# A hybrid encoder layer with expert retrieval: second token tile preloaded, ScalarE copies reordered, value sums on GpSimd for one stage, every fourth value block split

## The chip, the cores and the metric

One core of a Trainium2 chip runs the whole program. The metric is device time in microseconds (us) of one execution; the figure for the kernel before is the median of three runs. Engines are named as the profile names them: PE is TensorE (PEld its weight load), DVE is VectorE, ACT is ScalarE, POOL is GpSimd, SP is SyncE, which here only issues DMAs. "f32r" is a rounded form of float32; the kernel makes one float32 product from three f32r products of rounded parts and remainders.

## The reference, cut to what matters

The layer runs on two inputs of 256 tokens, `x_prompt` and `x_sample`: a short convolution and attention, then a retrieval over 16,384 experts, each a row `u` and a row `v` of 1024 numbers. The part that the change touches is the retrieval:

```python
def peer_ffn(x, wq, subkeys, u_tab, v_tab):
    q = (xf @ wq).reshape(T, PEER_HEADS, 2, PEER_HALF)
    s = jnp.einsum('thpc,hpnc->thpn', q, subkeys)
    sv, si = lax.top_k(s, PEER_TOPK)
    ...
    gates = jax.nn.softmax(cv, axis=-1)
    uc = jnp.take(u_tab, ic, axis=0)
    a = jax.nn.gelu(jnp.einsum('thkd,td->thk', uc, xc)) * gc
    vc = jnp.take(v_tab, ic, axis=0)
    return jnp.einsum('thk,thkd->td', a, vc)
```

Each token takes 8 heads x 16 experts = 128 experts. The result is added to the token's row `h`.

## The kernel before, in words

**Two ways to the same sum.** For `x_prompt` the kernel gathers: for each of two tiles of 128 tokens ("tile 1" is `t == 0`, "tile 2" is `t == 1`) and each of the 128 choices `k`, `g_issue` (L151) has POOL issue an indirect DMA of 128 rows `u|v`, 8 KB each (1.05 MB), into one of four ring places (`grow`). `g_dot` (L180) multiplies the u half with the tile's `x` row and sums it (DVE, 128x1024), `g_weight` (L171) puts Gelu and the gate on the sum (ACT, two operations on `dots`), `g_val` (L162) adds weight times v half to the tile's `h` row (DVE, 128x1024). That makes 256 gathers. A place is free for the next gather when its `g_val` is done. For `x_sample` the kernel is dense: it computes all 16,384 experts with matmuls and multiplies with a gate matrix that is mostly zero.

**Stages in order of the program.** (1) Layer front of `x_prompt`, its query projection and top-k. (2) Layer front of `x_sample`, with the first gathers beside it. (3) `projections` (L342) for `x_sample`, the "query projection": per head, two groups of 8 matmuls `pqq`, key scores `pn`, and `step1` (L815), which does the head's top-k on DVE, with sums of pairs (`cd`, L256 to L263) on POOL. (4) The "expert stage" (L913): 128 blocks `j`, each a 512 KB load of `u`, 8 matmuls into `pSj`, Gelu on ACT, which also frees the PSUM tile (four of them, `psS`). Beside it runs the generator `gates_dense` (L848): it finishes top-k, transposes the picks (`pi`, `pg`), then 64 times builds one-hot matrices for 4 tokens (DVE `oi`, `oj`, `gh`, ACT `gl`), multiplies them (`pgm`) and puts the gates into the matrix `A` (`Al`, `Ah`): where block `j` is done, DVE multiplies, where not, ACT copies. (5) The "value stage" (L939): 128 blocks, each a 512 KB load of `v` and 4 matmuls of 512 columns into `acc`; then the result is added to `h` and stored.

**What paces the gathers.** `bg(us)` (L221) is called after each group of matmuls and adds a share of `us` to a credit; 2.65 of credit (`GU`) buys one call of `gather` (L194), which does the oldest dot, an older value sum and the next issue. The shares are `SF` in stage 2, `SR` in stage 3 (through `step1`), `SS` in stage 4, where `SBS` is the share of `gates_dense`. In stage 5 what is left is spread evenly over the blocks. Each issue also waits for the last matmul emitted before it (`pe_mark`). The pacing is arithmetic on constants: it hands out 22, 18, 110 and 106 gathers to stages 2 to 5.

**What is where.** Weights, `u` and `v` come through SP's queue in program order, into four places `wtile` (and two more, `vp`, for every third `v`). The `x` and `h` rows of tile 1 stand in tiles `xg` and `hg` of the pool `gc`; when tile 1's last dot and last sum are done, POOL loads tile 2's rows into the same places (L189, L166 to L168). A scheduler under the tile framework decides the final order on each engine; each engine then runs its list in order, so whatever stands behind a waiting instruction waits as well.

Of the kernel before, what the change touches and what calls it, by code (L numbers as in the profile page):

```python
# [38 lines left out]
SR = 0.6  # L39
SS = 0.64  # L40
SMAX = 0.7
SBS = 0.42
# [3 lines left out]
def encoder_layer(ctx: ExitStack, tc: tile.TileContext, xp, xs_, meta, vec, w_in, w_out, wq,  # L46
# [33 lines left out]
    wp = ctx.enter_context(sb("wp", 4))  # L80
    selp = ctx.enter_context(sb("sel", 1, "right"))
    gc = ctx.enter_context(sb("gc", 1, "right"))
    ga = ctx.enter_context(sb("ga", GBUF, "right"))
# [21 lines left out]

    def wtile(name):
        return wp.tile([P, D], F32, tag="w", name=name)

    def weights(src, s, split=False):

        w = [wtile("w").rearrange("p (c n) -> p c n", c=4) for _ in range(2)]
        for q in range(2):
            nc.sync.dma_start(w[q], src[:, s, 4 * q:4 * q + 4])
        if not split:
            return lambda c, k=0: w[c // 4][:, c % 4]
        hl = [ga.tile([P, 2 * D], F32R, tag="g", name=n).rearrange("p (q x) -> p q x", q=2) for n in ("whi", "wlo")]
# [32 lines left out]
    ring = [ga] * GBUF  # L149
# [30 lines left out]
    def g_dot():  # L180
# [7 lines left out]
        if t == 0 and k == P - 1:  # L188
            x = gc.tile([P, D], F32, tag="xg", name="xg1")  # L189
            pool.dma_start(x, xdram)  # L190
            gctx["x"] = x
# [242 lines left out]
    def front(s, h, rn):  # L434
# [286 lines left out]
        if s == 0:  # L721
            for t in range(2):
                x = gc.tile([P, D], F32, tag="xg", name="xg0") if t == 0 else tmp.tile([P, D], F32, tag="xs", name="xs")
                dve.scalar_tensor_tensor(x, h[:, t, :], rn[:, t:t + 1], gf, op0=ALU.mult, op1=ALU.mult)
                xs2.append(x)
            gctx["x"] = xs2[0]
        if s == 0:
            hg = gc.tile([P, D], F32, tag="hg", name="hg0")
            pool.tensor_copy(hg, h[:, 0, :])
            gctx["h"] = hg  # L730
# [107 lines left out]

    share.update(a=SR, b=0.0)
    projections(xr1, sk1, sc1, q1, step1, rescale=rescale)  # L840
    pfs.close()
# [6 lines left out]
    def gates_dense():  # L848
# [4 lines left out]
        topk_left[0] = -1  # L853
        ogx = ExitStack()
# [7 lines left out]
        for t in range(2):  # L862
# [14 lines left out]
            for o in range(P // OC):  # L877
# [12 lines left out]
                for q in range(OC // 4):  # L890
# [8 lines left out]
                    for part, lo, hi in ((Al, 0, JH), (Ah, JH, P)):  # L899
                        m = min(max(n, lo), hi)  # L900
# [3 lines left out]
                        if m < hi:  # L904
                            act.activation(part[:, m - lo:hi - lo, a:a + 4], pj[:, m:hi], AF.Copy, scale=1.0 / GSH)
# [6 lines left out]
    ut = {}  # L912
    for j in range(P):  # L913
# [7 lines left out]
        n = tau[0]  # L921
        if n:
            act.activation(p[:, :n], p[:, :n], AF.Gelu)
            dve.tensor_tensor(A(j)[:, :n], p[:, :n], A(j)[:, :n], op=ALU.mult)
        if n < 256:
            act.activation(A(j)[:, n:], p[:, n:], AF.Gelu)
        r_done[0] = j + 1
        bg(3.5)
    run_tasks()

    vp = ctx.enter_context(sb("vp", 2, "right"))
# [4 lines left out]
    hd_ = gc.tile([P, 2, D], F32, tag="xr", name="hd")  # L936
    left = len(queue) + len(pend)
    done = 0
    for j in range(P):  # L939
        vb = vp.tile([P, D], F32, tag="v", name="v") if j % 3 == 2 else wtile("v")  # L940
        nc.sync.dma_start(vb, vn3[:, j])
        if j == P // 2:
            for t in range(2):
                act.dma_start(hd_[:, t, :], hdram[1 + t])
        for t in range(2):
            for q in range(2):
                i = pe.matmul(acc[t][q], A(j)[:, t * P:(t + 1) * P], vb[:, q * 512:(q + 1) * 512],  # L947
                              start=j == 0, stop=j == P - 1, skip_group_check=True)
        pe_mark[0] = i
        want = left * (j + 1) // (P - 2)  # L950
        while done < want:
            gather()
            done += 1
    while queue or pend or vals:
        gather()
# [73 lines left out]
```

## Time and profile before

| | us |
|---|---|
| median of three runs (1370.44 to 1372.22) | 1370.68 |
| the profiled execution | 1362.99 |
| its span | 1360.9 |
| PE busy in the span | 1298.1 |
| DVE busy | 1031.9 |
| ACT busy | 437.4 |
| POOL busy | 414.0 |

The profile is one execution. Its page gives busy time by engine and by group of instructions; views of the trace give the same for a stretch ("windows"), the waits ("who waited for whom"), the DMA traffic and the instructions in order of time. PE reaches 95% of the span, but the DMA engines are full for long stretches too, so what counts is which of them ends last in which stage. A plain float32 matmul shows as two records.

### The profile page before, as it was taken

To read this page: it belongs to the slowest core of one execution; us is meant where nothing else is said; L and a number is where in the kernel's file an instruction comes from. 1 tells how busy PE (TensorE), PEld (TensorE's weight loads), DVE (VectorE), ACT (ScalarE), POOL (GpSimd) and SP (SyncE) were. 2 spreads that over 40 slices of the span, in tenths; PEclk is the share of its full clock that TensorE was granted. 3 is DMA by queue.
4 is the path that set the end of the run, shared out by engine and by line. 5 is a ranking of instruction groups with operands and counts; after the bars stand their busy time and mean duration, and the time that the engine had idled before them with its cause. 6 is when DMAs were issued, how large, how long until landed. Compare 5 with 4: busy or idle time off the path is not lost. (4 is left out here: it accounts for less than half of the span.)

```text
span 1360.9 us, 17663 instructions
## 1 busy us (share of the span) xinstructions
PE 1298.1 (95%) x5870; PEld 927.9 (68%) x5870; DVE 1031.9 (76%) x2356; ACT 437.4 (32%) x1467; POOL 414.0 (30%) x480
## 2 busy tenths in 40 slices
PE   5999998998999887999999999999999999999998
PEld 5888986677888666888888888774443344444443
DVE  5656999776999889988888996676666665666665
ACT  4555533732221312555555543111111111111111
POOL 2111224331344342222221221223455523433331
PEclk9999999999999998999999999999999999999999
DMA  6434637577998999999999999999999999999997
GB/s 218 126 109 153 206 107 263 199 272 301 366 341 332 390 399 374 348 368 367 355 368 359 366 375 376 377 416 416 417 417 417 418 416 417 416 417 416 416 417 294
DMA packets 90234, 460.19 MB, mean 338 GB/s; under 512 B 10512, under 2 KB 11024, under 8 KB 57120
## 3 DMA queue, kind: packets, MB, share of 16 engines
q0 software_dynamic: 37296, 270.02, 49.7%
q1 hardware_dynamic: 50832, 182.33, 36.1%
q10 hardware_dynamic: 2016, 6.72, 1.3%
q8 instruction: 46, 0.75, 0.2%
q14 instruction: 44, 0.36, 0.1%
HBM read 454.81 MB, written 4.19 MB: 337 GB/s over the span
## 5 line engine op out<-in xcount | busy, mean ns | idle before, releaser
L157 POOL DMA_INDIRECT grow<-in_uv,eidx x256 | 331.9, 1297 | 694.8 <-PE acc L947 118.1
L130 PE MATMUL pSj<-xr,u 128*128 128x256 f32 x2048 | 465.6, 385 | 12.6 <-ACT Al L63 10.5
L130 PEld LDWEIGHTS pSj<-xr,u 128*128 128x128 f32 x2048 | 386.3, 192 | 68.7 <-ACT Al L63 14.5
L63 DVE SCALAR_TENSOR_TENSOR grow<-grow,xg 128x1024 f32<-128x1024 f32 x256 | 312.5, 1221 | 143.6 <-DMA grow<-in_uv,eidx 138.6
L63 DVE SCALAR_TENSOR_TENSOR hg<-grow,dots,hg 128x1024 f32<-128x1024 f32 x256 | 327.9, 1281 | 77.4 <-ACT dots L63 67.9
L947 PE MATMUL acc<-v,Al 128*128 128x512 f32 x752 | 329.9, 596 | 1.8
L947 PEld LDWEIGHTS acc<-v,Al 128*128 128x128 f32 x752 | 140.6, 190 | 190.6 <-issue 164.2
L63 ACT ACTIVATE dots<-dots 128x1 f32<-128x1 f32 x256 | 51.6, 202 | 552.2 <-DVE grow L63 551.2
L947 PE MATMUL acc<-v,Ah 128*128 128x512 f32 x272 | 118.0, 594 | 0.2
L947 PEld LDWEIGHTS acc<-v,Ah 128*128 128x128 f32 x272 | 51.3, 190 | 66.7 <-issue 62.1
L63 ACT ACTIVATE gl<-oj,glo 128x128 f16<-128x128 f16 x256 | 88.8, 393 | 10.9 <-DVE oj L63 5.1
L63 ACT ACTIVATE dots<-dots,gate_all 128x1 f32<-128x1 f32 x256 | 75.1, 294 | 7.5 <-ACT dots L63 0.6
L63 DVE TENSOR_TENSOR wlo<-w,whi 128x1024 fp32r<-128x1024 f32 x42 | 51.0, 1217 | 19.9 <-ACT whi L63 13.9
L63 ACT ACTIVATE pSj<-pSj 128x256 f32<-128x256 f32 (+39 forms) x94 | 26.6, 284 | 110.7 <-PE pSj L130 110.7
L130 PE MATMUL pqq<-xr,w 128*128 128x256 f32 x256 | 59.5, 385 | 0.7 <-DMA w<-in_wq 0.7
L130 PEld LDWEIGHTS pqq<-xr,w 128*128 128x128 f32 x256 | 48.2, 194 | 7.3 <-DMA w<-in_wq 1.1
L63 ACT ACTIVATE whi<-w 128x1024 fp32r<-128x1024 f32 x42 | 43.9, 1055 | 20.5 <-PE pqq L130 9.5
L130 PE MATMUL pc<-xT,w 128*128 128x258 f32 (+1 forms) x192 | 47.5, 390 | 1.1 <-DVE rb L63 0.6
L130 PEld LDWEIGHTS pc<-xT,w 128*128 128x128 f32 x192 | 34.9, 192 | 8.6 <-issue 2.5
L130 PE MATMUL pqq<-xr,whi 128*128 128x256 f32 x128 | 37.2, 292 | 0.0
L130 PE MATMUL pqq<-xrl,whi 128*128 128x256 f32 x128 | 36.4, 285 | 0.3 <-DVE xrl L63 0.3
L894 PE MATMUL pgm<-gh,oi 128*128 128x128 f16 x256 | 35.5, 219 | 1.3 <-DVE gh L63 1.3
(268 smaller groups left out, 1539.3 us busy)
## 6 DMA issues: line engine op xcount, KB each, us to landing
u<-in_u_t SPq DMA_DIRECT2D x128, 512.0 KB, 6.8
v<-in_v_n SPq DMA_DIRECT2D x128, 512.0 KB, 14.9
w<-in_w_in SPq DMA_DIRECT2D x36, 512.0 KB, 4.3
w<-in_wq SPq DMA_DIRECT2D x32, 512.0 KB, 5.0
w<-in_w_out SPq DMA_DIRECT2D x16, 512.0 KB, 4.8
grow<-in_uv,eidx POOLq DMA_INDIRECT x256, 9.2
hdram<-h ACTq DMA_DIRECT2D x3, 512.0 KB, 3.0
h<-in_xp SPq DMA_DIRECT2D x2, 512.0 KB, 7.3
```

Source lines behind the costliest of these rows:

```text
L63: i = f(*a, **k)
L130: i = pe.matmul(out, st_(c, a), mv(c, b), start=(n == 0), stop=(n == NC * len(terms) - 1))
L157: i = pool.indirect_dma_start(out=r, out_offset=None, in_=uv, in_offset=bass.IndirectOffsetOnAxis(ap=eidx[:, t, k:k + 1], axis=0))
L894: pe.matmul(pg[:, r, :], oi[:, k, :], gh[:, k, :], start=True, stop=False)
L947: i = pe.matmul(acc[t][q], A(j)[:, t * P:(t + 1) * P], vb[:, q * 512:(q + 1) * 512], start=j == 0, stop=j == P - 1, skip_group_check=True)
```

## The change

- Tile 2's rows: the ring gets five places of 8 KB. One, `ga[0]`, first holds tile 1's `x` and `h`; when the first gather of tile 2 is issued, a free ring place is taken for tile 2's `x` and `h`, POOL loads them there, and `ga[0]` joins the ring. `xg` and `hg` go.
- Stage 3: `SR` goes from 0.6 to 0.7. The value sum becomes two operations: ACT scales the v half in place by the weight, POOL adds it to the `h` row.
- Stage 4: `SBS` goes from 0.42 to 0.38, and a `yield 4.0` stands ahead of the transposes. Gelu and product of block `j` are emitted after the matmuls of block `j + 1`. In `gates_dense` both ACT copies are emitted ahead of both DVE products.
- Stage 5: `v` comes in pairs of blocks (1 MB, 8 KB a row) into three places, which take the room of `wtile`. Every fourth block (`SPL`) is split: ACT rounds its `A` and `v` to f32r, DVE makes the two remainders, and PE does three f32r products in place of one float32 product. The `h` rows of `x_sample` are loaded after the last `v`, by SP, in place of halfway, by ACT.

The pacing arithmetic now hands out 22, 21, 109 and 104 gathers to stages 2 to 5.

```diff
-SR = 0.6
+SR = 0.7
-SBS = 0.42
+SPL = 4
+SBS = 0.38
...
+    def row_pair():
+        p = ring_free.pop(0).tile([P, 2 * D], F32, tag="g", name="xh")
+        return p[:, :D], p[:, D:]
...
         t, k = queue.pop(0)
+        if t == 1 and k == 0:
+            ring_free.append(ring.pop(0))
+            gctx["next"] = row_pair()
+            pool.dma_start(gctx["next"][0], xdram)
+            pool.dma_start(gctx["next"][1], hdram[0])
+            ring.append(ga[0])
...
         t, k, r = vals.pop(0)
-        dve.scalar_tensor_tensor(gctx["h"], r[:, D:], dots[:, k:k + 1], gctx["h"], op0=ALU.mult, op1=ALU.add)
+        if on_pool[0]:
+            act.activation(r[:, D:], r[:, D:], AF.Copy, scale=dots[:, k:k + 1])
+            pool.tensor_tensor(gctx["h"], r[:, D:], gctx["h"], op=ALU.add)
+        else:
+            dve.scalar_tensor_tensor(gctx["h"], r[:, D:], dots[:, k:k + 1], gctx["h"], op0=ALU.mult, op1=ALU.add)
         if t == 0 and k == P - 1:
             pool.dma_start(yp[0:P, :], gctx["h"])
-            h = gc.tile([P, D], F32, tag="hg", name="hg1")
-            pool.dma_start(h, hdram[0])
-            gctx["h"] = h
+            gctx["h"] = gctx["next"][1]
...
+    on_pool[0] = True
     projections(xr1, sk1, sc1, q1, step1, rescale=rescale)
+    on_pool[0] = False
...
         topk_left[0] = -1
+        yield 4.0
...
-                    for part, lo, hi in ((Al, 0, JH), (Ah, JH, P)):
-                        m = min(max(n, lo), hi)
+                    parts = [(part, lo, hi, min(max(n, lo), hi)) for part, lo, hi in ((Al, 0, JH), (Ah, JH, P))]
+                    for part, lo, hi, m in parts:
+                        if m < hi:
+                            act.activation(part[:, m - lo:hi - lo, a:a + 4], pj[:, m:hi], AF.Copy, scale=1.0 / GSH)
+                    for part, lo, hi, m in parts:
                         if m > lo:
                             ...
-                        if m < hi:
-                            act.activation(part[:, m - lo:hi - lo, a:a + 4], pj[:, m:hi], AF.Copy, scale=1.0 / GSH)
...
+        late.append((j, p))
+        if len(late) > 1:
+            experts(*late.pop(0))
         bg(3.5)
+    experts(*late.pop(0))
...
-    vp = ctx.enter_context(sb("vp", 2, "right"))
+    wpx.close()
+    vp = ctx.enter_context(sb("vp", 3, "right"))
...
+    def values(j):
+        if j % 2 == 0:
+            vpair[0] = vp.tile([P, 2, D], F32, tag="v", name="v")
+            nc.sync.dma_start(vpair[0], vn3[:, j:j + 2])
+        vb = vpair[0][:, j % 2]
+        if j % SPL != SPL - 1:
+            return ((A(j), vb),)
+        vh, vl = vhl[:, 0], vhl[:, 1]
+        ...
+        act.activation(ah, A(j), AF.Copy)
+        act.activation(vh, vb, AF.Copy)
+        dve.tensor_tensor(al, A(j), ah.bitcast(F32), op=ALU.subtract)
+        dve.tensor_tensor(vl, vb, vh.bitcast(F32), op=ALU.subtract)
+        return ((ah, vh), (al, vh), (ah, vl))
```

How the order on the engines moves is shown at three places. The first is POOL in the query projection, one head (L157 and L179 are the issue of a gather, `cd` the pair sums that DVE's top-k waits for). Before:

```order
L157 DMA grow<-in_uv,eidx 128x2048
L259 TENSOR_TENSOR cd<-Al 128x2x16
L157 DMA grow<-in_uv,eidx 128x2048
L259 TENSOR_TENSOR cd<-Al 128x2x8
L259 TENSOR_TENSOR cd<-Al 128x2x5
L259 TENSOR_TENSOR cd<-Al 128x2x4
L259 TENSOR_TENSOR cd<-Al 128x2x3
L260 TENSOR_TENSOR cd<-Al 128x2x6
L263 TENSOR_TENSOR cd<-Al 128x2x8
```

POOL in the query projection now, one head (`xh` is the `h` row, L188 the new add):

```order
L179 DMA grow<-in_uv,eidx 128x2048
L188 TENSOR_TENSOR xh<-grow,xh 128x1024
L179 DMA grow<-in_uv,eidx 128x2048
L188 TENSOR_TENSOR xh<-grow,xh 128x1024
L281 TENSOR_TENSOR cd<-Al 128x2x16
L281 TENSOR_TENSOR cd<-Al 128x2x8
L281 TENSOR_TENSOR cd<-Al 128x2x5
L281 TENSOR_TENSOR cd<-Al 128x2x4
L281 TENSOR_TENSOR cd<-Al 128x2x3
L282 TENSOR_TENSOR cd<-Al 128x2x6
L285 TENSOR_TENSOR cd<-Al 128x2x8
```

An add of 1024 columns now stands behind each issue, and the pair sums stand behind the adds.

The second place is PE in the expert stage, where the transposes of the picks stand in the list (8 `pSj` make one block). Before:

```order
L130 MATMUL pSj<-xr,u 128x256 x256
L864 LDWEIGHTS idx_i
L864 MATMUL pi<-ident_4995,idx_i 128x128
L865 LDWEIGHTS idx_j
L865 MATMUL pi<-ident_4995,idx_j 128x128
L867 MATMUL pg<-ident,gate_all 128x128
L130 MATMUL pSj<-xr,u 128x256 x16
```

PE at the same place now:

```order
L137 MATMUL pSj<-xr,u 128x256 x312
L887 LDWEIGHTS idx_i
L887 MATMUL pi<-ident_5164,idx_i 128x128
L888 LDWEIGHTS idx_j
L888 MATMUL pi<-ident_5164,idx_j 128x128
L890 MATMUL pg<-ident,gate_all 128x128
L137 MATMUL pSj<-xr,u 128x256 x8
```

The transposes stand behind 39 blocks in place of 32.

The third place is SP's queue between the expert and the value stage. Before:

```order
L918 DMA u<-in_u_t 128x1024 x115
L941 DMA v<-in_v_n 128x1024 x2
L918 DMA u<-in_u_t 128x1024 x13
L941 DMA v<-in_v_n 128x1024 x126
L956 DMA out_yp<-hg_7901 128x1024
```

SP now:

```order
L954 DMA u<-in_u_t 128x1024 x128
L980 DMA v<-in_v_n 128x2048 x64
L1008 DMA hd<-hdram 128x2x1024
L1011 DMA out_yp<-xh 128x1024
L1016 DMA out_ys<-hd 128x512 x2
```

Two `v` loads used to go out ahead of the last 13 `u` loads. Now all 64 pairs stand behind the last `u`, and the built program makes the first pair wait for the last one-hot matmul of the expert stage (L918).

## Rows read from the trace of the kernel before

**Rows 1.** The page's first line.

```profile
span 1360.9 us, 17663 instructions
```

**Rows 2.** Windows: query projection, expert stage, value stage; us, busy by engine (records), PE clock, DMA share, GB/s.

```profile
331.00:401.00 70.00, 65.75 (x326) 57.20 (x325) 62.45 (x271) 19.02 (x68) 29.16 (x49) 0.98 0.93 346
401.00:907.00 506.00, 484.07 (x2569) 418.05 (x2568) 429.40 (x925) 205.21 (x817) 134.30 (x138) 0.99 0.96 371
907.00:1357.00 450.00, 447.94 (x1027) 192.00 (x1025) 288.41 (x346) 56.73 (x228) 168.75 (x111) 1.00 1.00 409
```

**Rows 3.** DMA view of 907 to 1340 us: traffic, and loads of v and gathers to landing.

```profile
DMA packets 33733, 180.42 MB, mean 417 GB/s; under 512 B 3736, under 2 KB 3736, under 8 KB 19703
## 3 DMA queue, kind: packets, MB, share of 16 engines
q0 software_dynamic: 15760, 114.79, 64.0%
q1 hardware_dynamic: 17667, 64.36, 37.1%
...
v<-in_v_n SPq DMA_DIRECT2D x123, 512.0 KB, 15.1
```

**Rows 4.** Waits from 907 to 1357 us: us in total, times, longest.

```profile
POOL grow L157 <- DMA grow<-in_uv,eidx: 97.1, 50, 3.7
...
PEld acc L947 <- DMA v<-in_v_n: 30.8, 40, 0.9
```

**Rows 5.** Windows of 20 us, columns as in Rows 2.

```profile
440.00:460.00 20.00, 15.83 (x66) 13.33 (x65) 16.74 (x28) 7.33 (x20) 4.98 (x5) 0.91 0.95 365
460.00:480.00 20.00, 18.36 (x83) 15.22 (x82) 16.83 (x28) 6.33 (x17) 6.76 (x6) 1.00 1.01 414
480.00:500.00 20.00, 18.64 (x83) 15.12 (x83) 17.00 (x27) 3.84 (x15) 8.36 (x6) 1.00 1.00 393
500.00:520.00 20.00, 16.54 (x69) 13.96 (x68) 18.67 (x29) 4.27 (x18) 7.96 (x5) 0.91 1.01 407
520.00:540.00 20.00, 11.96 (x50) 10.04 (x50) 18.12 (x30) 4.38 (x17) 5.65 (x5) 0.84 0.98 384
600.00:620.00 20.00, 20.00 (x123) 17.45 (x122) 17.30 (x38) 11.46 (x48) 4.22 (x4) 1.00 0.97 372
840.00:860.00 20.00, 19.29 (x101) 16.58 (x99) 8.75 (x17) 3.33 (x15) 2.37 (x2) 1.00 0.91 357
```

**Rows 6.** Waits from 400 to 907 us.

```profile
ACT dots L63 <- DVE grow L63: 138.7, 44, 7.6
...
POOL hg L168 <- DMA out_yp<-hg: 9.3, 1, 9.3
```

**Rows 7.** Timeline of 536 us: start, duration, engine, what, idle before it and releaser.

```profile
536.17 0.22 DVE L63 CAST ident<-ident 128x128 f16<-128x128 f32 x1
...
536.44 0.27 PE L864 MATMUL pi<-ident,idx_i 128*128 128x128 f16 x1 [8.04 <-DVE ident L63]
```

**Rows 8.** Groups by line: busy us, mean ns of one, idle before.

```profile
L157 POOL DMA_INDIRECT grow<-in_uv,eidx x256 | 331.9, 1297 | 694.8 <-PE acc L947 118.1 <-DMA grow<-in_uv,eidx 114.1 <-DVE Al L63 102.7
L63 DVE SCALAR_TENSOR_TENSOR hg<-grow,dots,hg 128x1024 f32<-128x1024 f32 x256 | 327.9, 1281 | 77.4 <-ACT dots L63 67.9 <-DMA hg<-hdram 9.3
...
L63 ACT ACTIVATE whi<-w 128x1024 fp32r<-128x1024 f32 x42 | 43.9, 1055 | 20.5 <-PE pqq L130 9.5 <-PE pc L130 3.2 <-PE po L130 3.0
...
L729 POOL COPY hg<-h 128x1024 f32<-128x1024 f32 x1 | 1.0, 1041 | 20.3 <-DVE h L63 20.3
```

**Rows 9.** Timeline in the query projection: two equal POOL operations, and DVE beside the first.

```profile
390.72 1.27 DVE L63 SCALAR_TENSOR_TENSOR hg<-grow,dots,hg 128x1024 f32<-128x1024 f32 x1
...
390.73 1.36 POOL L259 TENSOR_TENSOR cd<-Al 128x32 f32<-128x32 f32 x1
...
402.80 0.25 POOL L259 TENSOR_TENSOR cd<-Al 128x32 f32<-128x32 f32 x1
```

**Rows 10.** Timeline of PE in the first input's split query projection: two f32r matmuls in a row.

```profile
142.55 0.28 PE L130 MATMUL pqq<-xr,whi 128*128 128x256 f32 x1
142.67 0.28 PE L130 MATMUL pqq<-xrl,whi 128*128 128x256 f32 x1
```

More of the change, by code (lines that the diff above doesn't have):

```diff
@@ L79, in encoder_layer @@
     drm = ctx.enter_context(tc.tile_pool(name="drm", bufs=1, space=DRAM))
-    wp = ctx.enter_context(sb("wp", 4))
     selp = ctx.enter_context(sb("sel", 1, "right"))
     gc = ctx.enter_context(sb("gc", 1, "right"))
-    ga = ctx.enter_context(sb("ga", GBUF, "right"))
+    ga = [ctx.enter_context(sb(f"ga{i}", 1, "right")) for i in range(GBUF + 1)]
+    wpx = ExitStack()
+    wp = wpx.enter_context(sb("wp", 4, "right"))
     ident = cst.tile([P, P], F32, name="ident")
@@ L104, in rsqrt @@
         pool.tensor_tensor(out, stats, mhalf[:stats.shape[0], :n], op=ALU.pow)
+    spl = [0]
     def wtile(name):
@@ L115, in weights @@
             return lambda c, k=0: w[c // 4][:, c % 4]
-        hl = [ga.tile([P, 2 * D], F32R, tag="g", name=n).rearrange("p (q x) -> p q x", q=2) for n in ("whi", "wlo")]
+        k = 1 + 2 * spl[0]
+        spl[0] = 1 - spl[0]
+        hl = [ga[k + i].tile([P, 2 * D], F32R, tag="g", name=n).rearrange("p (q x) -> p q x", q=2)
+              for i, n in enumerate(("whi", "wlo"))]
         for q in range(2):
@@ L148, in encoder_layer @@
     gctx = {}
-    ring = [ga] * GBUF
+    ring = ga[1:]
+    on_pool = [False]
+    def row_pair():
+        p = ring_free.pop(0).tile([P, 2 * D], F32, tag="g", name="xh")
+        return p[:, :D], p[:, D:]
+    ring_free = [ga[0]]
     def g_issue():
@@ L188, in g_dot @@
         if t == 0 and k == P - 1:
-            x = gc.tile([P, D], F32, tag="xg", name="xg1")
-            pool.dma_start(x, xdram)
-            gctx["x"] = x
+            gctx["x"] = gctx["next"][0]
         vals.append((t, k, r))
@@ L721, in front @@
         if s == 0:
+            gctx["x"], gctx["h"] = row_pair()
             for t in range(2):
-                x = gc.tile([P, D], F32, tag="xg", name="xg0") if t == 0 else tmp.tile([P, D], F32, tag="xs", name="xs")
+                x = gctx["x"] if t == 0 else tmp.tile([P, D], F32, tag="xs", name="xs")
                 dve.scalar_tensor_tensor(x, h[:, t, :], rn[:, t:t + 1], gf, op0=ALU.mult, op1=ALU.mult)
                 xs2.append(x)
-            gctx["x"] = xs2[0]
         if s == 0:
-            hg = gc.tile([P, D], F32, tag="hg", name="hg0")
-            pool.tensor_copy(hg, h[:, 0, :])
-            gctx["h"] = hg
+            pool.tensor_copy(gctx["h"], h[:, 0, :])
             act.dma_start(hdram[0], h[:, 1, :])
@@ L911, in encoder_layer, with experts @@
     share.update(a=SS, b=SBS)
-    ut = {}
+    late = []
+    def experts(j, p):
+        n = tau[0]
+        if n:
+            act.activation(p[:, :n], p[:, :n], AF.Gelu)
+        if n < 256:
+            act.activation(A(j)[:, n:], p[:, n:], AF.Gelu)
+        if n:
+            dve.tensor_tensor(A(j)[:, :n], p[:, :n], A(j)[:, :n], op=ALU.mult)
+        r_done[0] = j + 1
     for j in range(P):
@@ L920, in encoder_layer @@
         mm(p, lambda c, k: ub[:, c * P:(c + 1) * P], xr1)
[L921 to L927, printed above, removed]
+        late.append((j, p))
+        if len(late) > 1:
+            experts(*late.pop(0))
         bg(3.5)
+    experts(*late.pop(0))
     run_tasks()
-    vp = ctx.enter_context(sb("vp", 2, "right"))
+    wpx.close()
+    vp = ctx.enter_context(sb("vp", 3, "right"))
+    ap_ = ctx.enter_context(sb("ap", 1, "right"))
     psgx.close()
@@ L935, in encoder_layer @@
     vn3 = v_n.rearrange("(i j) d -> i j d", j=P)
-    hd_ = gc.tile([P, 2, D], F32, tag="xr", name="hd")
+    vhl = gc.tile([P, 2, D], F32R, tag="xr", name="vhl")
     left = len(queue) + len(pend)
     done = 0
+    vpair = [None]
+    def values(j):
[6 more added lines that the diff above has]
+        vh, vl = vhl[:, 0], vhl[:, 1]
+        ah = ap_.tile([P, 256], F32R, tag="ah", name="ah")
+        al = ap_.tile([P, 256], F32R, tag="al", name="al")
+        act.activation(ah, A(j), AF.Copy)
[3 more added lines that the diff above has]
+        return ((ah, vh), (al, vh), (ah, vl))
+    nxt = values(0)
     for j in range(P):
-        vb = vp.tile([P, D], F32, tag="v", name="v") if j % 3 == 2 else wtile("v")
-        nc.sync.dma_start(vb, vn3[:, j])
-        if j == P // 2:
+        terms = nxt
+        nxt = values(j + 1) if j + 1 < P else None
+        for n, (a, v) in enumerate(terms):
             for t in range(2):
[L944 to L948, printed above, removed]
+                for q in range(2):
+                    i = pe.matmul(acc[t][q], a[:, t * P:(t + 1) * P], v[:, q * 512:(q + 1) * 512],
+                                  start=j == 0 and n == 0, stop=j == P - 1 and n == len(terms) - 1, skip_group_check=True)
         pe_mark[0] = i
@@ L953, in encoder_layer @@
             done += 1
+    hd_ = vp.tile([P, 2, D], F32, tag="v", name="hd")
+    nc.sync.dma_start(hd_, hdram[1:3].rearrange("t p d -> p t d"))
     while queue or pend or vals:
```

## The prediction

> **What bounds the kernel now.** I read the stages first. Cut at the first `pSj` and the first `acc` matmul, the windows show that the query projection takes 70 us, the expert stage 506 and the value stage 450 of the 1360.9 us [rows 1, 2]. Nothing before them is changed.
>
> In the value stage PE is busy 447.9 of 450 us [rows 2], which looks like a PE bound. The DMA view tells more: from 907 to 1340 us the DMA engines move 417 GB/s, and the shares of the two large queues add up to 101% [rows 3]. PE waits for `v` only 30.8 us, in 40 pieces of at most 0.9 us, and POOL's issues wait for gathers, which I read as waits for places whose gather lands late [rows 4]. So two resources end at almost the same time here. Taking PE time away uncovers the DMA engines and little else.
>
> In the expert stage the DMA engines move 371 GB/s, below the 417 they can do, and PE is busy 484.1 of 506 us [rows 2]. From 540 us on the 20 us windows look like the one at 600 us: PE 20.00 of 20. The idle time lies in the five windows from 440 to 540 us: 4.2, 1.6, 1.4, 3.5 and 8.0 us, with the granted clock at 0.91, 0.91 and 0.84 in three of them [rows 5], means of its two levels, 2.4 GHz and the 1.2 GHz that it falls to where PE has stood. The last piece is one wait: the transposes stand in PE's list, and PE waits 8.04 us until DVE has cast the identity they need [rows 7]. The other pieces (10.6 us together) come from gathers that are late: ACT waits for the dots 138.7 us in all [rows 6], and the Gelu that frees PE's tiles stands behind them in ACT's list. The gathers are late because DVE was full before: 62.45 of 70 us in the query projection [rows 2].
>
> **The change, part by part.** The profiled execution took 1362.99 us; the sum is made against that. The median of the runs is 7.7 us (0.6%) above it, and I subtract the same sum there. A measurement of this kernel can tell some 0.2% (2.7 us) from no change.
>
> *Transposes 7 blocks later.* PE reaches them behind 39 blocks in place of 32. At 484.1/128 = 3.8 us of PE time a block [rows 2] that gives DVE some 26 us more for what PE waited 8.04 us for [rows 7]. I count the whole wait, and 2 of the (1 - 0.84) x 20 = 3.2 us of clock missing in that window [rows 5]: **-10**. Ends: 0, if DVE is later by those 26 us, and -11. The one-hot work now lasts to the last block; its matmuls are the same, so PE pays nothing more.
>
> *Sums to ACT and POOL in the query projection.* DVE loses 18 sums of 1.28 us and gains 3 dots of about the same length [rows 8]: 62.45 - 23 + 4 = 43 of 70 us. ACT gains 21 scalings; the nearest row is its 128x1024 copy, 1.06 us [rows 8]: 19 + 22 = 41 us, not on the path. POOL gains 3 issues of 1.3 us and 21 adds. No row has a 1024-column add on POOL. The nearest is its copy of 1024 columns, 1.04 us [rows 8], the lower end; an add reads two inputs, so I take twice that, 2.08. POOL comes to 29.2 + 4 + 21 x 1.04 to 2.08 = 55 to 77 of 70 us [rows 2]. At 77 POOL has taken DVE's place as the late one, but late by less. Queued behind an add are the next issue and the pair sums that DVE's top-k waits for. There are also three more gathers (3.1 MB) to fit in. I take half of the 10.6 us of idle PE time: **-5**. Ends: -14 (all of it, and two clock dips of 1.8 us) and +10.6 (twice the loss), since the rows also show the two engines getting in each other's way: an equal pair sum takes 0.25 us alone, and 1.36 us where DVE started a product with two inputs 0.01 us before it [rows 9].
>
> The Trainium skill has a rule for this row ("SBUF — State Buffer", section "Who interferes with whom"): a VectorE instruction with two SBUF inputs and a GpSimd instruction that reads SBUF exclude each other for the whole instruction. The row agrees. By the skill's "GPSIMD Engine Reference", section 3.1, an add of 2048 float32 columns takes 4497 ns; halved, an estimate of 2.25 us, which would put POOL at 80 us in place of 77 and leave the sum as it is.
>
> *Gelu a block later, copies ahead of products.* ACT no longer waits for the matmuls of the block it has just been handed, but a late gather now holds up the Gelu one block sooner. These pull against each other, and from 540 us on PE has no idle time to win [rows 5]: 0.
>
> *Tile 2's rows ahead.* Before, POOL stood 9.3 us for the store of tile 1 before it could load tile 2's `h` [rows 6], and PE lost 0.7 us in that window [rows 5]. **-1** (0 to -2). Now the fourth issue of tile 2 waits for that store, with three gathers in flight to cover it.
>
> *Value stage.* PE first. A block of 4 float32 matmuls costs 8 records of 447.9/1024 = 0.437 us, 3.5 us [rows 2]. A split block has 12 f32r matmuls; at 256 columns they follow each other in 0.12 us [rows 10], so at 512 I take 0.24, 2.9 us. 32 blocks x 0.6 = 20 us, PE needs 428. Then the DMA engines bind. They moved 409 GB/s x 450 us = 184.0 MB in the stage [rows 2]. Two gathers fewer take off 2.1 MB; the five `v` blocks that used to be issued before the stage (123 of 128 lie in the window [rows 3]) come back in, 2.6 MB, because the first pair now waits for the last one-hot matmul. That is 184.5 MB, 442.4 us at 417 GB/s. Longer rows help: a packet of the gather queue took 16 x 433 x 0.640 / 15760 = 0.281 us, one of SP's queue, with half the bytes, 16 x 433 x 0.371 / 17667 = 0.145 [rows 3]. Two short ones cost 0.010 us more than a long one; 8192 such pairs over 16 engines are 5.0 us. So 437.4, plus 2 us until the first pair flows and 6 for PE's last two blocks after the last bytes: 445 against 450. **-5**. PE's wait for the first pair (half as much took 15.1 us to land under load [rows 3]) and the 1.1 + 1.3 us that each split puts on ACT and DVE (the sizes of the copy and of a two-input product [rows 8]), fit into the 17 us that PE has over and DVE's 38% idle time [rows 2]. Ends: -13 (PE's own 428 plus 9) and +42 (below).
>
> Sum: -10 - 5 - 1 - 5 = **-21**: 1342.0 for a profiled execution, 1349.7 for the median.
>
> **The rivals.** (a) *GpSimd becomes the bound of the query projection.* If every add also waits out a DVE product, as the pair sum did (1.1 us [rows 9]), POOL needs 33 + 21 x 3.2 = 100 of 70 us, the gathers come later than before, and the second term turns from -5 to +7. For it: the exclusion in the rows. Against it: 18 of the products that collided are gone from DVE. Sum -9: 1361.7. The same lock that the skill states would act here.
>
> (b) *The value stage is no longer kept full, and the kernel is slower.* Place: ACT and DVE in the value stage. A split's conversions wait for a `v` pair to land, and the dots of the gathers stand behind them in the same lists. With three places for pairs a pair is sent out four blocks (some 14 us) before use, while half as much took 15.1 us to land [rows 3]. If the ring of gathers stands full and unread meanwhile, the rate falls toward that of the expert stage, 371 GB/s [rows 2], where the stage would take 184.5/0.371 = 497 us, less 5, +42. At 390 GB/s, between the two, it takes 473 + 8 = 481, +31, and the sum is +15: 1385.7. It decides below 184.5/(466 - 8) = 403 GB/s, where the other terms are eaten up. Against it: PE waits for the same pair at the same time, and while it does, two to three pairs are in flight, so the engines have work.
>
> (c) *All the stalls go.* -11, -14, -2, and -13 in the value stage: -40, 1330.7. For it: nothing but late work held PE in those windows.
>
> (d) *Nothing comes of it*: POOL's lateness takes back what the transposes and the DMA give, 1370.7.
>
> **How the numbers follow.** Forecast 0.55, its own range 1341 to 1358; (a) 0.17; (b) 0.12; (c) 0.11; (d) 0.05. The range from 1331 to 1367 takes in the forecast, (a) and half of (c), and leaves out (b) and (d): 0.78. Faster by over 0.2%: 0.55 + 0.17 + 0.11 = 0.83; the same 0.05; slower 0.12.
>
> **What would show each step.** Transposes: the wait of PE for DVE's cast gone. Sums: POOL's new adds near 2 us, PE's idle time from 440 to 540 us about halved; if the adds take over 3 us and ACT's waits for dots grow, it is (a). Value stage: PE busy well under the stage's length, waits for `v` well above 30.8 us, DMA still near 417 GB/s up to the end; under 403 it is (b). Wrong altogether would be an expert stage as long as before, or a PE that still never waits for `v`.

## The result, and the profile after

The changed kernel is **slower**: median 1382.49 us (1372.42 to 1387.01, 20 runs) against 1365.8 (1359.88 to 1372.22, 20 runs) for the kernel before on the same chip; ratio 1.0111, 95% interval 1.0093 to 1.0129. By the ratio that is 15 us more where I forecast 21 less, and outside the range. The profiled execution after took 1387.01 us, the slowest of its runs, the one before 1362.99, below its median: the traces differ by 24, not 15.

The three stages of the kernel after, in windows (columns as in [rows 2]):

```profile
334.80:425.60 90.80, 70.73 (x327) 58.65 (x325) 75.30 (x356) 37.45 (x91) 68.82 (x75) 0.93 0.88 320
425.60:947.50 521.90, 489.55 (x2566) 421.18 (x2567) 429.51 (x845) 207.85 (x830) 155.41 (x139) 0.97 0.94 360
947.50:1378.90 431.40, 422.79 (x1151) 217.60 (x1152) 309.49 (x385) 93.79 (x277) 124.29 (x104) 1.00 1.00 413
```

Against [rows 2] the query projection takes 91 us in place of 70, the expert stage 522 in place of 506, the value stage 431 in place of 449 (both cut at the start of the last `acc` matmul, behind which the span goes on for 4.4 us before and 6.4 after). The query projection also starts 3.6 us later; in the other kernels of this document, whose work up to there is much the same, its start lies between 330.4 and 335.9 us, so I read nothing into that. All three stages moved much further than my terms, and in different directions.

**Query projection.** Groups by line and form of that stage: busy us, mean ns of one, idle before.

```profile
L188 POOL TENSOR_TENSOR xh<-grow,xh 128x1024 f32<-128x1024 f32 x15 | 36.0, 2397 | 7.5 <-ACT grow L64 7.3
L64 DVE SCALAR_TENSOR_TENSOR grow<-grow,xh 128x1024 f32<-128x1024 f32 x15 | 27.8, 1852 | 6.1 <-DMA grow<-in_uv,eidx 6.1
L179 POOL DMA_INDIRECT grow<-in_uv,eidx x16 | 19.6, 1223 | 15.9 <-issue 10.4 <-PE pqq L137 2.6 <-POOL xh L188 1.9
L64 ACT ACTIVATE grow<-grow,dots 128x1024 f32<-128x1024 f32 x16 | 18.3, 1147 | 0.9
```

One add takes 2.40 us; I took 2.08. And DVE's product, which took 1.21 us in this stage before (the same group of the kernel before: 12 products, mean 1207 ns), takes 1.85 beside the adds. The waits of the kernel after from 334 to 426 us:

```profile
ACT dots L64 <- DVE grow L64: 38.0, 13, 7.0
PEld pn L372 <- ACT qs L64: 19.7, 10, 4.6
PE pn L372 <- ACT qs L64: 15.7, 10, 4.3
...
DVE grow L64 <- DMA grow<-in_uv,eidx: 6.1, 6, 2.0
...
DVE Al L64 <- POOL cd L281: 1.6, 1, 1.6
```

PE now stands 15.7 us for ACT's copy `qs` of the queries; in the trace before only its weight load waits for that copy, 0.7 us. The copy stands in ACT's list behind the weights of the gathers (`dots`) and the new scalings, and these wait for DVE's product. One such round in the timeline of the kernel after (start, us, engine, what):

```profile
384.87 2.37 POOL L188 TENSOR_TENSOR xh<-grow,xh 128x1024 f32<-128x1024 f32 x1
...
386.44 1.88 DVE L64 SCALAR_TENSOR_TENSOR grow<-grow,xh 128x1024 f32<-128x1024 f32 x1
...
388.36 0.20 ACT L64 ACTIVATE dots<-dots 128x1 f32<-128x1 f32 x1 [2.68 <-DVE grow L64]
...
388.98 1.15 ACT L64 ACTIVATE grow<-grow,dots 128x1024 f32<-128x1024 f32 x1
...
390.03 0.36 ACT L64 ACTIVATE qs<-pqq 128x256 f32<-128x256 f32 x1
...
390.45 0.71 PE L372 MATMUL pn<-Ah,qs 128*128 128x128 f32 x4 [0.23 <-ACT qs L64]
```

The product begins beside an add and ends 1.08 us after the add's end (388.32 against 387.24). The adds themselves are held up little: 14 of the 15 take 2.34 to 2.38 us, and one, which began during a product, takes 2.92. So DVE's longer products are one thing that holds DVE, and so the stage; the waits above give two more, late gathers (6.1 us) and pair sums (1.6 us). How full GpSimd is shows in the chain that ended last, from 370 to 410 us (start, us, what):

```profile
by line: POOL xh L188 35.5%; DMA grow<-in_uv,eidx 24.3%; POOL grow L179 19.6%; POOL cd L281 13.0%; issue 7.5%; POOL cd L282 4.2%; DVE Al L64 3.0%; POOL cd L285 1.8%; DVE s L64 1.3%; POOLq L188 0.2%; POOLq L179 0.1%
...
371.74 1.69 POOL cd L281 x4
...
373.91 0.96 POOL grow L179
...
374.89 2.36 POOL xh L188
...
377.52 1.66 POOL grow L179
...
379.19 2.37 POOL xh L188
...
381.72 1.67 POOL cd L281 x4
```

From one set of pair sums to the next are 9.98 us: two issues (2.6), two adds (4.7), the pair sums (2.0), and little between. For some 30 us the chain never leaves GpSimd. By an estimate from this round, eight heads at 10 us are 80 us. DVE has no room either: in the four windows of 10 us from 370 to 410 us it is busy 9.62, 9.55, 8.81 and 9.34 us, GpSimd 9.54, 9.53, 9.53 and 9.24.

**Expert stage.** PE's waits in the kernel after from 410 to 945 us:

```profile
PE pgm L917 <- DVE gh L64: 17.4, 3, 8.2
PE pSj L137 <- ACT Al L64: 9.6, 9, 4.6
PE pn L372 <- ACT qs L64: 8.8, 3, 4.3
```

The wait of the transposes [rows 7] is gone. A wait for `gh`, the next thing that DVE makes for PE, stands in its place, 8.13 us at 591, and a second one, 8.16 us, stands at 871, where the gathers change from tile 1 to tile 2.

**Value stage.** DMA view of the kernel after, 960 to 1370 us:

```profile
DMA packets 23767, 172.42 MB, mean 421 GB/s; under 512 B 2624, under 2 KB 2624, under 8 KB 2834
...
v<-in_v_n SPq DMA_DIRECT2D x60, 1024.0 KB, 9.4
```

The rate is 421 GB/s in place of 417 [rows 3]. But the windows also count POOL's issues: 104 gathers fall in this stage, 111 before [rows 2]. A gather is 1.05 MB, 2.5 us at 421 GB/s; seven of them are 17.5 us, as much as the stage has gained. (e4 and e12 show below that it takes the split as well.) Over the whole run both kernels move the same 460.2 MB.

### The profile page after: what moved, and what is told of

Read it like the earlier page. It is cut to its first block, busy times and chain, and to the rows that moved or that the text cites. A ratio compares the mean times of both kernels' runs of the same rounds, so it can differ in the third digit from the quotient of the medians.

```text
span 1385.3 us, 18082 instructions
## 1 busy us (share of the span) xinstructions
PE 1288.5 (93%) x5998; PEld 961.8 (69%) x5998; DVE 1068.1 (77%) x2403; ACT 496.3 (36%) x1554; POOL 429.3 (31%) x501
## 4 chain that ended last, share of the span: by engine, by line
PE 36%; DMA 25%; DVE 8%; issue 3%; POOL 3%; ACT 0%; DVEq 0%; POOLq 0%; SPq 0%
DMA grow<-in_uv,eidx 24%; PE pSj L137 21%; PE acc L1000 13%; DVE grow L64 2%; DVE xh L64 2%; POOL xh L188 1%; DVE Al L64 1%; PE pgm L917 1%; PE pgm L918 1%; DVE Ah L64 1%; DMA out_yp<-xh 1%; POOL grow L179 1%; DVE vhl L64 1%; POOL cd L281 0%; DMA Ah<-in_skT 0%
## 5 line engine op out<-in xcount | busy, mean ns | idle before, releaser
L179 POOL DMA_INDIRECT grow<-in_uv,eidx x256 | 301.8, 1179 | 712.8 <-DVE xh L64 163.5
L64 DVE SCALAR_TENSOR_TENSOR grow<-grow,xh 128x1024 f32<-128x1024 f32 x256 | 327.3, 1278 | 138.0 <-DMA grow<-in_uv,eidx 137.4
L64 DVE SCALAR_TENSOR_TENSOR xh<-grow,dots,xh 128x1024 f32<-128x1024 f32 x235 | 301.2, 1282 | 56.9 <-ACT dots L64 56.7
L1000 PE MATMUL acc<-v,Al 128*128 128x512 f32 x568 | 249.7, 596 | 5.0 <-DMA v<-in_v_n 5.0
L1000 PEld LDWEIGHTS acc<-v,Al 128*128 128x128 f32 x568 | 108.5, 191 | 132.7 <-issue 130.7
L1000 PE MATMUL acc<-v,Ah 128*128 128x512 f32 x200 | 87.3, 592 | 0.0
L1000 PE MATMUL acc<-vhl,ah 128*128 128x512 f32 x256 | 82.1, 442 | 0.0
L64 DVE TENSOR_TENSOR wlo<-w,whi 128x1024 fp32r<-128x1024 f32 x42 | 50.9, 1216 | 18.6 <-PE pc L137 11.3
L1000 PEld LDWEIGHTS acc<-vhl,ah 128*128 128x128 f32 x256 | 48.2, 188 | 23.2 <-issue 13.2
L188 POOL TENSOR_TENSOR xh<-grow,xh 128x1024 f32<-128x1024 f32 x21 | 50.7, 2413 | 12.3 <-ACT grow L64 7.7
L917 PE MATMUL pgm<-gh,oi 128*128 128x128 f16 x256 | 36.2, 222 | 17.4 <-DVE gh L64 17.4
L64 DVE TENSOR_TENSOR gh<-oj,dup 128x512 f16<-128x512 f16 x64 | 27.0, 422 | 30.7 <-PE pgm L917 29.8
```

What stands on the lines that cost most here:

```text
L64: i = f(*a, **k)
L188: pool.tensor_tensor(gctx["h"], r[:, D:], gctx["h"], op=ALU.add)
L917: pe.matmul(pg[:, r, :], oi[:, k, :], gh[:, k, :], start=True, stop=False)
L1000: i = pe.matmul(acc[t][q], a[:, t * P:(t + 1) * P], v[:, q * 512:(q + 1) * 512], start=j == 0 and n == 0, stop=j == P - 1 and n == len(ter ...
```

## The experiments

A table first; its times of stages come from the profiled executions, cut as above, with the gathers issued in each. "QP" is the query projection.

| kernel | QP us | expert us (gathers) | value us (gathers) | ratio to before, 95% |
|---|---|---|---|---|
| before | 70.0 | 506.1 (113) | 449.2 (111) | |
| after | 90.8 | 521.9 (116) | 431.4 (104) | 1.0111 (1.0093 to 1.0129) |
| e1 | 80.0 | 518.7 (117) | 431.3 (104) | 1.0018 (0.9996 to 1.0039) |
| e2 | 86.2 | 520.4 (116) | 430.6 (104) | 1.0087 (1.0063 to 1.0112) |
| e3 | 76.0 | 502.8 (112) | 447.2 (111) | 1.0006 (0.9986 to 1.0026) |
| e4 | 86.1 | 523.6 (116) | 442.1 (104) | 1.0172 (1.0140 to 1.0204) |
| e5 | 89.2 | 519.8 (115) | 432.1 (105) | 1.0087 (1.0057 to 1.0117) |
| e6 | 89.9 | 515.1 (111) | 448.7 (111) | 1.0194 (1.0161 to 1.0227) |
| e7 | 72.9 | 515.5 (120) | 426.6 (104) | 0.9920 (0.9894 to 0.9947) |
| e8 | 75.2 | 517.3 (115) | 432.6 (106) | 1.0000 (0.9974 to 1.0025) |
| e9 | 70.3 | 517.7 (114) | 446.3 (110) | 1.0016 (0.9995 to 1.0038) |
| e10 | 72.0 | 521.8 (121) | 422.9 (102) | 0.9925 (0.9896 to 0.9954) |
| e11 | 71.7 | 528.1 (127) | 426.8 (97) | 1.0083 (1.0053 to 1.0113) |
| e12 | 75.1 | 516.5 (121) | 439.0 (102) | 1.0050 (1.0026 to 1.0074) |

Seven of these have the query projection of the kernel before unchanged (before, e3, e7, e9 to e12): 70 to 76 us, so 5 us of a stage in a single profile mean nothing. A ratio of 0.001 is 1.4 us.

**e1: the sums back on DVE**, the rest as in the kernel after.

```diff
-    on_pool[0] = True
```

> The kernel after, with the sums of the query projection back on DVE, everything else as changed. Theory A (the scalings on ACT and the adds on GpSimd hold GpSimd and so the gathers, the copies and PE's weight transposes, 91 us of query projection in place of 70): the query projection falls to 70 to 76 us, GpSimd is busy under 12 of 20 us there, and the kernel is 15 to 20 us faster than the kernel after: 1362 to 1367, a ratio to the kernel before of 0.996 to 1.000. Rival (the query projection is longer because of the larger share of gathers given to it and the changed ring places): it stays above 84 us and the time stays within 5 us of the kernel after. Rival 2: it falls to 75 us, but the expert stage gets the backlog and grows by as much, no gain.

Measured: 1.0018 against 1.0111, 12.7 us faster than the kernel after. Theory A holds in its direction; the size is short of my 15 to 20, and 80 us remain in the query projection of this profile. (The share of gathers is still 0.7 there, but e8 has the same share and 75.2 us.) POOL's busy time in the stage falls from 68.82 to 31.75 us:

```profile
335.90:415.90 80.00, 67.77 (x328) 59.34 (x327) 68.89 (x287) 19.94 (x72) 31.75 (x52) 0.94 0.90 336
```

The chain moves with the sums. In the kernel after, from 345 to 425 us, GpSimd's adds hold 23.5% of it and ACT's scalings 1.4%; in e1, from 350 to 415 us, DVE's operations hold most of it (`Al` 32.8%, `grow` 17.4%, `xh` 16.5%) and GpSimd's pair sums 2.6%. No run separates the adds from the scalings; that the adds are the costly half rests on these shares.

**e6: the sums alone**, in the kernel before, with its share of 0.6.

```diff
+        if on_pool[0]:
+            act.activation(r[:, D:], r[:, D:], AF.Copy, scale=dots[:, k:k + 1])
+            pool.tensor_tensor(gctx["h"], r[:, D:], gctx["h"], op=ALU.add)
+        else:
...
+    on_pool[0] = True
     projections(xr1, sk1, sc1, q1, step1, rescale=rescale)
+    on_pool[0] = False
```

> The kernel before, with the sums of the query projection as scalings on ACT and adds on GpSimd, the share of gathers left at 0.6. Theory A (the scalings stand in ACT's list ahead of the copies that PE's transposed scores need, and GpSimd is full): the query projection grows by 6 to 12 us, PE's waits for `qs` are there, and the kernel is 8 to 13 us slower than before: ratio 1.006 to 1.010. Rival (only the larger share 0.7 filled GpSimd; at 0.6 it has room): ratio 0.996 to 1.002.

Measured: 1.0194, 26.5 us slower than before, twice the top of what I expected, and the rival falls: at the old share GpSimd has no room either (67.87 us busy in a stage of 89.9, with the same 16 gathers in it as in the kernel after). The groups of its query projection show the same prices as the kernel after. Its waits from 410 to 945 us, in the second piece below, show another bill: PE stands 15.9 us in one wait for one-hot work.

```profile
L168 POOL TENSOR_TENSOR hg<-grow,hg 128x1024 f32<-128x1024 f32 x14 | 34.5, 2465 | 11.5 <-ACT grow L63 11.4
L63 DVE SCALAR_TENSOR_TENSOR grow<-grow,xg 128x1024 f32<-128x1024 f32 x16 | 31.8, 1985 | 1.7 <-DMA grow<-in_uv,eidx 1.7
```

```profile
PE pgm L902 <- DVE gh L63: 19.0, 2, 15.9
```

**e2: no preload** (tile 2's rows loaded as before, four ring places).

```diff
-            gctx["next"] = row_pair()
-            pool.dma_start(gctx["next"][0], xdram)
-            pool.dma_start(gctx["next"][1], hdram[0])
-            ring.append(ga[0])
...
-            gctx["h"] = gctx["next"][1]
+            h = gc.tile([P, D], F32, tag="hg", name="hg1")
+            pool.dma_start(h, hdram[0])
+            gctx["h"] = h
```

> The kernel after, with tile 2's rows loaded as in the kernel before and four ring places throughout. Theory B (the fourth gather of tile 2 goes into the place that tile 1's y still holds, and GpSimd stands 11.5 us behind the store with no gather in flight): the wait of PE for DVE at about 870 us (8.2 us) is gone, and the kernel is 7 to 10 us faster than the kernel after: 1372 to 1375. Rival (the old wait for the store, 9.3 us on GpSimd, comes back and costs as much): within 3 us of the kernel after.

Measured: 1.0087, 3.3 us faster than the kernel after, with intervals that overlap, so not told from no gain. Theory B falls: the wait at the change of tile stays. Waits from 850 to 880 us in e2:

```profile
DVE hg L64 <- DMA hg<-hdram: 8.9, 1, 8.9
...
PE pgm L915 <- DVE gh L64: 7.1, 1, 7.1
```

And the same place in the kernel after, from its timelines of POOL and of PE (start, us, instruction, idle before it):

```profile
850.44 0.58 POOL L192 DMA_DIRECT2D out_yp<-xh  x1
862.51 1.66 POOL L179 DMA_INDIRECT grow<-in_uv,eidx  x1 [11.49 <-DVE Ah L64]
...
871.14 0.27 PE L917 MATMUL pgm<-gh,oi 128*128 128x128 f16 x1 [8.16 <-DVE gh L64]
```

With the preload DVE waits there for a gather that started late: its issue stands 11.49 us behind the store of tile 1's result, whose place it is to fill. (The bracket names a DVE operation; in the chain that ended last it is the store, issued at 850.44, that takes 11.30 us to land.) Without the preload DVE waits for tile 2's row. PE loses 7 to 8 us either way; e5 asks whether that is because one-hot work is still going on.

**e5: no delay of the one-hot work** in the kernel after.

```diff
-SBS = 0.38
+SBS = 0.42
...
-        yield 4.0
```

> The kernel after without the delay of the one-hot work (no extra step of 4.0 ahead of it, its share back from 0.38 to 0.42); the Gelu a block later and the copies ahead of the products stay. Theory D (the delay only moves PE's first wait from the transposes to the first one-hot matmul, and it stretches the one-hot work over the change of tile, where DVE's late gathers now stop PE a second time, 8.2 us at 871): the second wait goes, the first stays at about 8 us under either name, PE's waits for `gh` fall from 17.4 to under 10 us, and the kernel is 7 to 10 us faster than the kernel after, ratio to the kernel before 1.004 to 1.006. Rival (the second wait belongs to the change of tile and hits PE whatever the one-hot work's place): within 3 us of the kernel after, 1.009 to 1.013.

Measured: 1.0087, 3.3 us faster, intervals overlapping: near the rival's outcome. The one-hot matmuls now run from 570 to 883 us in place of 591 to 942, but that is still past the change of tile, and PE's waits for `gh` are 18.2 us in place of 17.4. In the kernel before they run from 545 to 845, where the store of tile 1's result goes out at 837, and wait 1.3 us in all, none of it there. The other profiles agree in the main: where one-hot work ends within 9 us of that store (before, e3, e6, e9), PE waits for no `gh` behind it; where it goes on, PE waits there for 6 to 14 us in eight of them, though only for some 4 in e7 and e12.

**e3: the value stage alone**, in the kernel before.

```diff
-        vb = vp.tile([P, D], F32, tag="v", name="v") if j % 3 == 2 else wtile("v")
-        nc.sync.dma_start(vb, vn3[:, j])
...
+            vpair[0] = vp.tile([P, 2, D], F32, tag="v", name="v")
+            nc.sync.dma_start(vpair[0], vn3[:, j:j + 2])
...
+        return ((ah, vh), (al, vh), (ah, vl))
```

> The kernel before, with the value stage of the kernel after alone (v in pairs with rows of 8 KB, one block in 4 split). Theory C (the value stage by itself gains the 16 us that the two traces show, and nothing else of the change touches it): 1350 us, ratio 0.988, value stage 432 to 437 us. My term of the forecast: 445 us, ratio 0.996. Rival (the gain is there because the stage began later with a fuller ring, or the boundary gives it back): ratio 0.996 to 1.002.

Measured: 1.0006, nothing; theory C falls, the third outcome holds. With 111 gathers the stage takes 447.2 us and PE is busy only 426 of them (windows; the second piece is a wait of PE in the stage):

```profile
913.00:1360.20 447.20, 426.22 (x1152) 218.00 (x1151) 327.17 (x408) 96.61 (x291) 133.63 (x111) 0.99 0.99 412
...
930.00:950.00 20.00, 18.13 (x44) 10.08 (x45) 15.99 (x20) 4.62 (x13) 8.37 (x6) 0.83 0.91 356
```

```profile
PE acc L969 <- ACT vhl L64: 7.5, 1, 7.5
```

Once it runs, the engines move some 421 GB/s; at its start they do not (356 GB/s from 930 to 950 us, PE 7.5 us before the first split block), and its end is 1.9 us longer (6.3 us from the last `acc` start to the end of the span, before 4.4). These two are some 3.1 us (20 us x (1 - 356/421)) and 1.9 us, an estimate, and return what the longer rows give (4.1 us, below).

**e4: no split** in the kernel after (`SPL = 1000`, pairs kept).

> The kernel after with no block split: v still comes in pairs of 8 KB rows. If the longer rows alone carry the value stage's gain (DMA bound): value stage 434 to 440 us, time within 5 us of the kernel after. If PE binds once the DMA is faster: 448 to 450 us of PE work remain, value stage 448 to 452, the kernel is 14 to 17 us slower than the kernel after: 1396 to 1400.

Measured: 1.0172, 8.3 us slower than the kernel after, between the two outcomes that I had written, and so is the stage, 442.1 us. PE fills the stage to the end, so with 104 gathers it is PE that binds, and the split pays:

```profile
940.10:1382.20 442.10, 442.10 (x1023) 195.54 (x1024) 269.86 (x323) 52.70 (x212) 124.53 (x104) 0.99 0.99 404
```

**e7 and e12: more gathers in the expert stage**, with the new value stage (e7, on e3) and with the old one (e12, on the kernel before). The edit is the same:

```diff
-SS = 0.64
+SS = 0.685
```

> The kernel before with the value stage of the kernel after, and the share of gathers in the expert stage raised from 0.64 to 0.685, so that some 8 of the 111 gathers of the value stage come in the expert stage instead. Theory E (the value stage is bound by the bytes: the split pays only where gathers are taken out of it, 2.5 us each, and the expert stage's DMA engines, at 371 GB/s, have room for them): the value stage falls from 449 to 430 to 435 us, the expert stage grows by less than 6, and the kernel is 10 to 18 us faster than the kernel before: ratio 0.987 to 0.993. Rival (DVE is what holds the gathers in the expert stage, so that every one that is moved there costs its 2.5 us again): ratio 0.998 to 1.004.

> The kernel before with the share of gathers in the expert stage raised from 0.64 to 0.685 alone, the value stage as before. Theory E (without the split PE's 448 us hold the value stage, so that fewer gathers there win nothing, and the expert stage pays 9 us for them): value stage 446 to 450, ratio 1.004 to 1.008. Rival (the share alone is what gains, and the new value stage has no part in it): ratio 0.991 to 0.995.

Measured: e7 0.9920, 10.9 us under the kernel before; only it and e10, which adds a delay to it, beat both kernels. e12 1.0050. Alone, the value stage gives 1.0006 and the share 1.0050; together they are 0.9920, 18.6 us less than the sum of the two. The last two stages of e7, then of e12:

```profile
407.40:922.90 515.50, 486.06 (x2568) 419.48 (x2566) 444.56 (x947) 208.86 (x831) 142.29 (x146) 0.98 0.97 377
922.90:1349.50 426.60, 421.37 (x1152) 217.70 (x1152) 309.38 (x386) 93.24 (x277) 117.80 (x104) 1.00 1.00 414
```

```profile
407.00:923.50 516.50, 489.00 (x2569) 423.41 (x2568) 448.95 (x953) 210.74 (x835) 141.92 (x147) 0.97 0.97 381
923.50:1362.50 439.00, 439.00 (x1025) 194.62 (x1023) 265.78 (x319) 52.13 (x210) 121.85 (x102) 1.00 0.99 399
```

In e12 PE is busy 439.0 of 439.0 us and the DMA engines drop to 399 GB/s; in e7 both are nearly full. Theory E holds in its times, but not in its sizes. I expected a value stage of 446 to 450 us for e12, and it fell by 10.2 to 439.0: PE's 447.9 busy us before [rows 2] held some 9 us of waiting, since the same matmuls need 439.0 here. The split alone shortens the stage by 2.0 us, until the DMA engines bind; fewer gathers alone by 10.2, until PE binds; both by 22.6. The gathers cost the expert stage some 10 us (9.4 in e7, 10.4 in e12), so only both together leave a gain.

**e11: share 0.73** (`SS = 0.73`, `SMAX = 0.75`, else as e7).

> The kernel with the value stage, its share of gathers in the expert stage raised further from 0.685 to 0.73 (and the cap beside it from 0.70 to 0.75). Theory E: the value stage with some 96 gathers needs about 411 us of DMA time, but PE's 422 us now end it, so it falls by no more than 8 of the 431 us, while the expert stage pays some 1.2 us for each gather that it takes, 9 us: within 4 us of the kernel with 0.685, ratio 0.990 to 0.996. Rival (PE has more to give): another 8 us, ratio 0.986.

Measured: 1.0083, a miss to the slow side. The profile shows only a part of it, since it is the fastest of the six runs (1367.98 us, median 1377.6). In it the expert stage paid 12.6 us for 7 more gathers, 1.8 each in place of the 1.2 that I expected (DVE busy 459.23 of 528 us; PE waits 19.5 us in 10 pieces for `gh`), and the value stage did not fall: its DMA rate is 398 GB/s. Of the three shares tried with the new value stage (0.64, 0.685 and 0.73), that of e7 is the best.

**e8: the kernel after without three parts** (e1, e2 and e5 together).

> The kernel after without its sums on GpSimd, without the preload and without the delay of the one-hot work: what stays is the value stage, the share 0.7 in the query projection, the Gelu a block later and the copies ahead of the products. If the parts add up (12.7 us for the sums, 3.3 for the preload, 7 to 10 for the delay, each against the kernel after): 23 to 26 us faster than the kernel after, ratio to the kernel before 0.992 to 0.995. If they overlap (each frees what the next one holds): 0.998 to 1.003.

Measured: 1.0000, 15.2 us faster than the kernel after. The sums alone are 12.7 of these, and the three parts undone one by one make 19.3, so they overlap a little, or not at all within the noise. What stays of the change, the value stage and the share 0.7 among it, is worth nothing together.

**e9: Gelu a block later and copies ahead alone**, in the kernel before.

```diff
+        late.append((j, p))
+        if len(late) > 1:
+            experts(*late.pop(0))
```

> The kernel before, with the Gelu a block later and ACT's copies ahead of DVE's products, nothing else. My term for this was 0: ratio 0.998 to 1.002, expert stage 503 to 508 us. Theory F (this part is what is left of the longer expert stage, 517 us with 115 gathers where three other parts were undone, against 506 with 113 in the kernel before: a late Gelu lets PE run only with one score tile less in hand, and DVE stands before its products until ACT has made all copies): the expert stage takes 512 to 518 us and the kernel is 6 to 11 us slower, ratio 1.004 to 1.008.

Measured: 1.0016, between my 0 and theory F's price; the interval takes in no change and 5 us. Its expert stage is 517.7 us in the profile, but that execution was the slowest of its twelve (1375.13 us), so I leave open whether this part costs 0 or a few us.

**e10: the delay of 4.0 alone**, added to e7.

> The kernel with the value stage and the share 0.685 (0.992 of the kernel before), with the extra step of 4.0 ahead of the one-hot work added, nothing else. My term for it: PE's wait for the cast of the identity (13.1 us there) goes, 10 us gained: ratio 0.984 to 0.987. Theory D (DVE's lateness is a backlog that the next step meets again): PE waits 8 us or more for `gh` in its place, and the time stays within 3 us, 0.990 to 0.994.

Measured: 0.9925 against 0.9920, nothing. PE's wait for the cast falls from 13.1 to 2.5 us, and its waits for `gh` rise from 6.4 to 21.9 (waits from 405 to 960 us):

```profile
PE pgm L897 <- DVE gh L64: 21.9, 4, 12.7
...
PE pi L867 <- DVE ident L64: 2.5, 1, 2.5
```

## Why the prediction was wrong, by its own steps

**Sums to ACT and POOL: -5 forecast, +12.7 (e1 against the kernel after) to +26.5 (e6 against before) measured.** This is the step that turned the sign. The load that I worked out, 77 us, was even above the 68.82 that POOL shows, but only because I took 21 adds from the plan of the pacing; 15 ran in the stage, at 2.40 us. What failed is "late, but late by less": I compared 77 with DVE's old load, took DVE as relieved (43 us), and let the excess become late gathers, while the stage stayed at 70 us. In the trace both engines are nearly full for most of the stage, and the lateness does not stay with the gathers, it lengthens the stage to 90.8 us: the next issue stands behind an add, DVE's product waits for the add that it meets, ACT's `qs` stands behind weights that wait for the product, and PE's key scores wait for `qs` (15.7 us). The pair sums, which I had seen as queued behind the adds, held DVE only once, for 1.6 us. The two measured prices differ by 14 us; of e6's, 9.0 come in the expert stage, where PE stands 15.9 us for `gh`, and why that wait is so much longer there stays open. Rival (a) had this engine, but it too priced the result in late gathers (+7), and not by its reason: an add takes 2.40 us, not 3.2. The exclusion between the two engines did act; DVE paid for it. DVE does 12 sums fewer in this stage (14 before, 2 after), 15.2 us at 1.27 each, but its 15 dots cost 0.65 us more each, 9.7 us; with the top-k work that now also falls into the longer stage, it is busy 75.30 us where I had 43. The Trainium skill's rule ("SBUF — State Buffer", section "Who interferes with whom") also says that the order of issue decides which of the two is held up; the rows agree: GpSimd paid in the trace before [rows 9], DVE here.

**Transposes 7 blocks later: -10 forecast, 0 measured** (e10 +0.0005, e5 the other way about: undoing the delay gains 3.3 us with overlapping intervals). The step "gives DVE some 26 us more for what PE waited 8.04 us for" failed; its own end 0 came out, but not by the condition that I gave it ("if DVE is later by those 26 us"): the cast came in time, or nearly (2.5 us in e10), and `gh` came late. DVE's lateness is a queue of work, not an appointment.

**Tile 2's rows: -1 forecast**, 3.3 us slower measured, not told from 0 (e2). I wrote that three gathers in flight would cover the fourth issue; in the trace it stood 11.49 us and DVE ran dry. What goes with PE's loss at the change of tile is one-hot work beside it, with or without the preload (e2, e5); no run changes that alone.

**Gelu later, copies ahead: 0 forecast**, +0.0016 with an interval that takes in 0 (e9).

**Value stage: -5 forecast; 0 measured alone (e3), -18 in the trace of the kernel after.** That the DMA engines bind once the split frees PE was right, though they bound before it as well (PE needs 439.0 us for the old matmuls, e12, where I read 447.9). Its sizes were right too: 4 GB/s more from longer rows (5.0 us forecast, 180.4 MB at 421 in place of 417 make 4.1), and 19.3 us of PE time for 32 split blocks (442.10 in e4 less 422.79; 20 forecast). The term that was mis-sized is "two gathers fewer": I took it from the plan of the pacing, 106 to 104, where the trace had 111 in the stage [rows 2]. Seven fewer are 17.5 us. They were no gain either, since they came in the stages ahead: in e8 the value stage takes 432.6 us with 106 gathers, and the kernel is at 1.0000. Rival (b) did not occur: 413 GB/s held.

So the result is: sums +12.7 us, the preload and the delay together about +2.5 (15.2 less 12.7, not told from 0), and the rest together 0. What lengthens the expert stage to some 517 us in e8 and e9 stays open.

## What to carry to other kernels

Compare an engine's new load not with the old late engine but with the length of the stage, price what it does to the engine that it was taken from, and follow what stands behind it in every list: where other engines wait for small results there, its excess lengthens the stage itself. Where two resources end together, relieve both in one step and measure that: here each half alone was worth nothing or a loss (1.0006, 1.0050), and both were 0.9920. A wait that goes is not won until the next instruction from the same late engine comes in time, and a stage's gain counts only after the work that left it has been found elsewhere.

## What the runs showed of the hardware that I had not expected

- Where an add of 1024 float32 columns on GpSimd and a product of two inputs on DVE met, the later one waited for the other's end. Mostly that was DVE: the product took 1.85 us on average (1.99 in e6) where it took 1.21 without adds, while 14 of 15 adds took 2.34 to 2.38 us. What was moved off DVE was in good part paid for again on DVE.
- The DMA engines' rate with gathers and `v` together rose from 417 to 421 GB/s when `v`'s rows went from 4 to 8 KB (packets under 8 KB in the two windows: 19703 [rows 3] and 2834). In e3, with the mix of the kernel before (64.1% and 37.0% for the two large queues from 960 to 1345 us), it was 421 as well.
